# Up-projection of a ConvFFN: two buffers for a unit's evicted quarters, early history copies, the gated result in the tanh buffer, and put-off gates two units later

## The chip, the cores and the metric

The kernel runs on one core of one Trainium2 chip. The metric is the device time of one execution in microseconds (us); several executions are timed, and their median is quoted.

The core's engines, with the names that the profile uses: TensorE (PE; its weight loads are listed as PEld), VectorE (DVE), ScalarE (ACT), GpSimd (POOL) and SyncE (SP). Each takes its instructions in the order of its own queue. SyncE here only issues DMAs.

## The reference, cut to what matters

One layer: an input projection, an mLSTM group and an attention group, an output projection with a layer norm, then a ConvFFN with a layer norm. There are 2048 prompt tokens and 8 sequences of 16 new tokens, 1024 model columns and D_FF = 2816. The change lies in the ConvFFN:

```python
def conv_ffn(h, conv_prev, w_up, w_conv, b_conv, w_down):
    T = h.shape[1]
    u = h @ w_up                                    # value columns | gate columns, 2 * 2816
    ext = jnp.concatenate([conv_prev.astype(u.dtype), u], axis=1)
    c = b_conv + sum(ext[:, j:j + T] * w_conv[j] for j in range(CONV_W))   # causal, width 3
    a, g = jnp.split(c, 2, axis=-1)
    return (jax.nn.silu(g) * a) @ w_down, ext[:, -(CONV_W - 1):]
```

So each output token needs the two u rows before it: the history. For the prompt it comes from the token block before, for the 8 short sequences from a given state (`sconv`). All is computed in float32.

## The kernel before, in words

**Stages.** Input projection, mLSTM and attention chains woven with it, output projection, up-projection (`f_ups`), down-projection (`f_downs`). In the profile the up-projection lies at about 930 to 1900 us, the down-projection behind it.

**Loops of the up-projection.** Tokens are in three blocks b (`FBLOCKS`): 6, 6 and 5 tiles of 128 tokens; the last block holds four prompt tiles and the tile of the short sequences. In each block there are 22 units j (`NFF`), one for 128 value columns and the 128 gate columns that go with them. A unit (b, j) is computed as a Strassen-Winograd scheme of 2 x 2 blocks (value/gate columns by first/second half of the block's tokens): seven products s instead of eight. Each product is 12 matmuls (L1876): four steps of contraction, three matmuls for each, since float32 operands are split into a high and a low part (hh and hl for tokens, two halves of uw for weights). Products accumulate in three PSUM banks A, B and C. Units with even and odd j use different sets of banks, shown as fup and dps. The order of products is written out by hand: 6, 2, 5, product 1 of the next unit, 3, product 7 of the next unit, 4.

**Evictions (`f_after`, at most one set for each product).** For s = 1, ScalarE copies bank A to B (L1889). For s = 6, B is copied to a buffer u2 (L1901) before product 5 accumulates on B. For s = 2, A is copied into the tile u (L1903). For s = 5, B is copied to u4 (L1905), before product 3 accumulates on it, and VectorE adds u4 to bank C into u (L1906, and L1908 for the short sequences), before product 4 accumulates on C. For s = 3, B is copied into u (L1910, L1912). For s = 4, VectorE adds u2 to C into u (L1915). The tiles u, u2 and u4 have one buffer each.

**What follows in a unit, also in `f_after`.** GpSimd copies the history into the first two columns of u (L1916, and in block 2 L1918 for the short sequences), ScalarE computes the first tap of the convolution with its bias into cc (L1922), VectorE adds the other two taps (L1924; all three once for values and once for gates), and GpSimd saves the last two columns (L1925 to `prev`, L1927 to `convs`). In block 0 cc is stored to a DRAM buffer zc. In blocks 1 and 2 `f_gate` computes the gated result: tanh (L1946, into th), then two VectorE operations (L1947, L1948, the result into cc), then SyncE stores it to zf (L1949, L1951). Behind that, a put-off gate: the cc of a unit of block 0 is loaded back (L1939) and gated. This is done in units 0 to 17 of block 1 and in units 2 to 5 of block 2. The tile cc has two buffers, th has one.

**Work between the units.** `f_next` prepares the weights of later products: it casts the high part (ScalarE, L220) and subtracts it (VectorE, L221), stores what later blocks need again to zw, and loads it from there in blocks 1 and 2. At the turn of a block (the last unit of blocks 0 and 1) `f_tokens` forms the token operands hh and hl of the next block with the same L220 and L221 and some additions. `o_late` finishes two layer norms of the stage before, with a small tile of constants (`lnp`) in the pool f3.

**Down-projection.** `d_load` (L1993) loads the gated results from zf into tiles r, `d_weights` (L2011) loads the down weights (wdn, or sums of them, zt), `d_tokens` and the helper at L220/L221 split them, and `f_downs` runs the matmuls (L2080). The pools f2 (u, u2, u4 and four of the token operands) and f3 (`sconv`, `convs`, cc, th and others) are closed at its start and their space is given to r2, r3, r4 and yacc. `skew` only allocates padding, so that what follows lies at another address.

**Order.** TensorE's order is the program's order. For the other engines and for SyncE's DMAs a scheduler in the framework builds the queues from the program, so an edit can move instructions that it doesn't touch.

## Time and profile before

| | |
|---|---|
| timed runs | 2339.32, 2344.24 and 2351.91 us; median 2344.24 |
| profiled execution, its own time | 2340.57 us |
| its span in the profile | 2338.8 us |
| mean granted TensorE clock | 0.996 |
| TensorE busy | 2295.6 us (98%) |
| VectorE / ScalarE / GpSimd busy | 1803.8 (77%) / 1298.7 (56%) / 243.2 (10%) us |
| DMA | 624.98 MB, mean 267 GB/s |

The profile describes the profiled execution alone, in us from the start of its span. Busy times are sums over instructions. In rows of instructions the columns are start, duration, engine, line, operation, output <- inputs, shape, and in square brackets the idle time of the engine before the instruction, with what released it. In rows of windows they are the stretch and its length, the busy time of each engine with its number of instructions, the granted TensorE clock, the DMA engines' busy share, and GB/s. In rows of waits: who waited, for whom, total us, number of times, longest. In rows of groups: busy total and mean ns, then idle time before with what ended it. In rows of DMA issues: issues, KB each, median us from issue to landing.

### The profile page before, as it was taken

What the parts mean: (1) busy time and instruction counts of PE and PEld (TensorE: products, weight loads), DVE (VectorE), ACT (ScalarE), POOL (GpSimd) and SP (SyncE); (2) the same over time, 40 slices, a digit from 0 to 9 for tenths busy, and PEclk for the clock granted to TensorE, in tenths of its full rate; (3) what the DMA queues carried; (4) which work ended last, traced back from release to release, by engine and by line L of the source; (5) the groups of instructions that cost most, each with busy time, mean ns of one, the idle gap of its engine ahead of it and who ended that gap; (6) DMA issues with size and microseconds to landing.
All of it is one profiled execution on the core that took longest, in us unless ns stands there. A gap on an engine that the chain in (4) does not pass through costs nothing.

```text
span 2338.8 us, 39880 instructions
## 1 busy us (share of the span) xinstructions
PE 2295.6 (98%) x14425; PEld 2112.9 (90%) x14425; DVE 1803.8 (77%) x3150; ACT 1298.7 (56%) x2465; POOL 243.2 (10%) x298
## 2 busy tenths in 40 slices
PE   9999999999999999999999999999999999999998
PEld 8989998899887777999999999999999978888887
DVE  8676586796678898987788776778766777796897
ACT  5353466676666664655556455455545544554753
POOL 0101101101111221300001000002100100010100
PEclk9999999999999999999999999999999999999999
DMA  8798889889977667787776989878988776766763
GB/s 284 267 315 283 289 289 317 288 286 325 302 258 251 212 210 253 263 321 280 285 270 247 314 315 320 306 274 264 312 289 263 248 273 218 237 201 214 242 194 110
DMA packets 297365, 624.98 MB, mean 267 GB/s; under 512 B 47052, under 2 KB 140240, under 8 KB 297168
## 3 DMA queue, kind: packets, MB, share of 16 engines
q1 hardware_dynamic: 296304, 619.29, 77.7%
q10 hardware_dynamic: 864, 3.15, 0.4%
q8 instruction: 114, 1.87, 0.3%
q14 instruction: 83, 0.68, 0.1%
HBM read 451.78 MB, written 170.56 MB: 266 GB/s over the span
## 4 chain that ended last, share of the span: by engine, by line
PE 65%; DVE 9%; DMA 4%; ACT 3%; issue 3%; POOL 1%; SPq 0%; DVEq 0%; ACTq 0%; POOLq 0%
PE fup L1876 15%; PE dps L1876 15%; PE dps L2080 6%; PE fup L2080 6%; PE fht L2080 5%; PE dps L735 5%; PE dps L225 2%; DVE cc L1924 2%; PE dps L227 2%; PE dps L226 2%; DMA zf<-cc 1%; PE ppo L1371 1%; ACT cc L1922 1%; PE psc L1322 1%; DVE uw L221 1%
## 5 line engine op out<-in xcount | busy, mean ns | idle before, releaser
L1876 PE MATMUL dps<-hh,uw 128*128 128x384 f32 (+1 forms) x1848 | 479.1, 327 | 6.9 <-ACT u L1901 1.9
L1876 PE MATMUL fup<-hh,uw 128*128 128x384 f32 (+1 forms) x1848 | 477.5, 327 | 3.3 <-ACT u L1901 3.0
L1876 PEld LDWEIGHTS dps<-hh,uw 128*128 128x128 f32 x1848 | 329.3, 188 | 11.1 <-ACT u L1901 3.0
L1924 DVE SCALAR_TENSOR_TENSOR cc<-u,cw,cc 128x768 f32<-128x768 f32 (+1 forms) x264 | 252.5, 977 | 107.0 <-ACT cc L1922 102.2
L1876 PEld LDWEIGHTS fup<-hh,uw 128*128 128x128 f32 x1848 | 329.4, 188 | 4.9 <-ACT u L1901 3.8
L1876 PE MATMUL fup<-hl,uw 128*128 128x384 f32 (+1 forms) x924 | 301.3, 326 | 1.7 <-DVE hl L221 1.7
L1876 PE MATMUL dps<-hl,uw 128*128 128x384 f32 (+1 forms) x924 | 301.0, 326 | 0.0
L735 PE MATMUL dps<-w,oh 128*128 128x256 f32 x1344 | 253.8, 285 | 5.7 <-ACT zev L801 4.0
L221 DVE TENSOR_TENSOR w<-wraw,w 128x1024 fp32r<-128x1024 f32 (+2 forms) x163 | 188.2, 1160 | 61.2 <-ACT w L220 59.7
L220 ACT CAST w<-wraw 128x1024 fp32r<-128x1024 f32 (+2 forms) x163 | 161.0, 994 | 123.9 <-PE dps L735 58.8
L735 PEld LDWEIGHTS dps<-w,oh 128*128 128x128 f32 x1344 | 211.6, 190 | 18.1 <-issue 8.9
L220 ACT CAST uw<-wraw 128x1024 fp32r<-128x1024 f32 x126 | 123.4, 981 | 177.5 <-PE dps L2080 104.2
L1922 ACT ACTIVATE cc<-u,cw 128x768 f32<-128x768 f32 (+1 forms) x132 | 129.5, 997 | 122.2 <-DVE u L1915 62.2
L221 DVE TENSOR_TENSOR uw<-wraw,uw 128x1024 fp32r<-128x1024 f32 x126 | 142.4, 1131 | 64.9 <-ACT uw L220 64.8
L735 PE MATMUL dps<-w,ol 128*128 128x256 f32 x672 | 187.7, 279 | 0.0
L735 PE MATMUL dps<-oh,w 128*128 128x256 f32 x896 | 171.1, 284 | 5.8 <-ACT zev L801 1.6
L1876 PEld LDWEIGHTS fup<-hl,uw 128*128 128x128 f32 x924 | 173.5, 188 | 2.5 <-DVE hl L221 2.5
L1876 PEld LDWEIGHTS dps<-hl,uw 128*128 128x128 f32 x924 | 173.5, 188 | 0.0
L2080 PE MATMUL fup<-uw,fu 128*128 128x512 f32 x726 | 171.2, 392 | 2.0 <-DVE uw L221 2.0
L2080 PEld LDWEIGHTS fup<-uw,fu 128*128 128x128 f32 x726 | 137.2, 189 | 31.4 <-DVE uw L221 2.4
L2080 PE MATMUL dps<-uw,fu 128*128 128x512 f32 x660 | 160.7, 389 | 0.0
L735 PEld LDWEIGHTS dps<-oh,w 128*128 128x128 f32 x896 | 140.8, 188 | 12.4 <-issue 4.1
(337 smaller groups left out, 4621.1 us busy)
## 6 DMA issues: line engine op xcount, KB each, us to landing
uw<-zw SPq DMA_DIRECT2D x176, 512.0 KB, 4.9
zw<-uw SPq DMA_DIRECT2D x88, 512.0 KB, 3.0
w<-zws SPq DMA_DIRECT2D x72, 512.0 KB, 6.6
wv<-wup SPq DMA_DIRECT2D x66, 512.0 KB, 5.5
wraw<-wi SPq DMA_DIRECT2D x64, 512.0 KB, 5.2
wraw<-zt SPq DMA_DIRECT2D x60, 512.0 KB, 4.4
wraw<-wdn SPq DMA_DIRECT2D x45, 512.0 KB, 3.8
wraw<-wo SPq DMA_DIRECT2D x40, 512.0 KB, 4.6
```

Of the source, the lines that this page charges most:

```text
L220: nc.scalar.copy(hi, src)
L221: nc.vector.tensor_sub(lo, src, hi.bitcast(F32))
L225: mm(out, ah, bh, start=start, stop=False)
L226: mm(out, ah, bl, start=False, stop=False)
L227: mm(out, al, bh, start=False, stop=stop)
L735: mm(o, l, r, start=s in (1, 7) and c == k == i == 0, stop=k == 3 and i == 2, skip_group_check=True)
L1322: nc.tensor.matmul(ps[kvh][:, j, :nk], q[rs, j0 + j], k[rs, sel], start=i == 0, stop=i == 2)
L1371: nc.tensor.matmul(po[64 * kvh:64 * kvh + 64], w, pts[:, kvh], start=kt == 1, stop=kt == nk)
L1876: mm(ps, l[:, k], r[:, k], start=s in (1, 7) and k == 0 and i == 0, stop=k == 3 and i == 2, skip_group_check=True)
L1922: S.activation(c[:, v], u[:, v, 2:2 + n], AF.Identity, bias=w[3], scale=w[2])
L1924: V.scalar_tensor_tensor(c[:, v], u[:, v, i:i + n], w[i], c[:, v], op0=ALU.mult, op1=ALU.add)
L2080: mm(ps, l[:, k, c], r[:, k], start=s in (1, 4, 7) and u == 0 and k == 0 and i == 0, stop=u == nu - 1 and k == n - 1 and i == 2, skip_grou ...
```

## The change

- The tiles u, u2 and u4 get two buffers each instead of one.
- The two history copies of a unit are made when its tile u is allocated (at s = 6), not after its last eviction.
- The gated result is written over the tanh in th and stored from there, no longer written into cc; th gets two buffers.
- `sconv` and `convs` become the two halves of one tile `hist`. It is allocated in the middle of block 1, where the load of `sconv` moves too, and takes the place of the layer norm constants `lnp`.
- The put-off gates of block 0 are done in units 2 to 19 of block 1 instead of 0 to 17; those in block 2 stay.
- The padding behind the up-projection shrinks from 480 to 448 bytes per partition.

TensorE's instructions and their order are the same in both kernels, and each other engine has as many instructions as before.

```diff
--- before.py
+++ after.py
@@ -290,7 +290,7 @@
             self.f2, f2cm = enter("f2sb")
             self.f3, f3cm = enter("f3sb")
             self.f_ups(n)
-            self.skew(self.f2, 480)
+            self.skew(self.f2, 448)
             close(f3cm)
             close(f2cm)
             self.f2, f2cm = enter("dsb")
@@ -1672,7 +1672,7 @@
             yield
         for hf in range(2):
             c = slice(hf * 512, hf * 512 + 512)
-            gb = self.f3.tile([P, 2, 512], F32, name="lnp", tag="th", bufs=1)
+            gb = self.f3.tile([P, 2, 512], F32, name="lnp", tag="hist", bufs=1)
             for i, n in enumerate(("ln1_g", "ln1_b")):
                 nc.sync.dma_start(gb[:, i], self.a[n][:, c].to_broadcast([P, 512]))
             yield
@@ -1819,10 +1819,8 @@
 
     def f_ups(self, n):
         nc = self.nc
-        self.sconv, self.convs = [self.f3.tile([P, 2, NFF, DB, 2], F32, name=n_, tag=n_, bufs=1) for n_ in ("sconv", "convs")]
         for _ in range(AHEAD - n):
             self.f_next()
-        nc.sync.dma_start(self.sconv, self.a["sconv"].rearrange("p (v j) b r -> p v j b r", v=2))
 
         self.banks = [[pool.tile([P, 512], F32, name=n, tag=n) for _ in range(3)] for pool, n in ((self.fup, "fup"), (self.dps, "dps"))]
         self.f_written(0)
@@ -1835,6 +1833,10 @@
                 nxt = self.f_hT(b + 1)
             if i == 4:
                 self.f_written(1)
+            if (b, j, s) == (nb - 2, NFF // 2, 6):
+                hist = self.f3.tile([P, 2, 2, NFF, DB, 2], F32, name="hist", tag="hist", bufs=1)
+                self.sconv, self.convs = hist[:, 0], hist[:, 1]
+                nc.sync.dma_start(self.sconv, self.a["sconv"].rearrange("p (v j) b r -> p v j b r", v=2))
             self.f_product(b, j, s)
             while self.made < min(i + 1 + (AHEAD if b == 0 else AHEAD + 2), len(self.seq)):
                 self.f_next()
@@ -1891,8 +1893,11 @@
         if s == 7:
             return
         if s == 6:
-            u = f2.tile([P, 2, 770], F32, name="u", tag="u", bufs=1)
-            self.u = u, *[f2.tile([P, 384], F32, name=m, tag=m, bufs=1)[:, :h] for m in ("u2", "u4")]
+            u = f2.tile([P, 2, 770], F32, name="u", tag="u", bufs=2)
+            self.u = u, *[f2.tile([P, 384], F32, name=m, tag=m, bufs=k)[:, :h] for m, k in (("u2", 2), ("u4", 2))]
+            nc.gpsimd.tensor_copy(u[:, :, 0:2], self.prev[:, :, j])
+            if has_s:
+                nc.gpsimd.tensor_copy(u[:, :, 2 + WP:2 + n].rearrange("p v (b l) -> p v b l", b=DB)[:, :, :, 0:2], self.sconv[:, :, j])
         u, u2, u4 = self.u
         us = u[:, :, 2 + WP:2 + n].rearrange("p v (b l) -> p v b l", b=DB) if has_s else None
         m = WP - h
@@ -1913,9 +1918,6 @@
         if s != 4:
             return
         V.tensor_add(u[:, 1, 2:2 + h], C, u2)
-        nc.gpsimd.tensor_copy(u[:, :, 0:2], self.prev[:, :, j])
-        if has_s:
-            nc.gpsimd.tensor_copy(us[:, :, :, 0:2], self.sconv[:, :, j])
         c = self.f3.tile([P, 2, 768], F32, name="cc", tag="cc", bufs=2)[:, :, :n]
         for v in range(2):
             w = [self.cw[:, v * NFF + j, i:i + 1] for i in range(4)]
@@ -1932,7 +1934,7 @@
         self.f_gate(c, b, j, WP, n)
 
         i = (b - 1) * NFF + j
-        i = i if i < 18 else i - 6 if 24 <= i < 28 else None
+        i = i - 2 if 2 <= i < 20 else i - 6 if 24 <= i < 28 else None
         if b and i is not None:
             W0 = len(FBLOCKS[0]) * P
             c = self.f3.tile([P, 2, 768], F32, name="cc", tag="cc", bufs=2)[:, :, :W0]
@@ -1942,14 +1944,14 @@
     def f_gate(self, c, b, j, WP, n):
         nc, V = self.nc, self.nc.vector
         W = len(FBLOCKS[b]) * P
-        th = self.f3.tile([P, 768], F32, name="th", tag="th", bufs=1)[:, :n]
+        th = self.f3.tile([P, 768], F32, name="th", tag="th", bufs=2)[:, :n]
         nc.scalar.activation(th, c[:, 1], AF.Tanh, scale=0.5)
         V.scalar_tensor_tensor(th, th, 1.0, c[:, 1], op0=ALU.add, op1=ALU.mult)
-        V.tensor_mul(c[:, 0], th, c[:, 0])
-        nc.sync.dma_start(self.zf[b][j, :, :WP], c[:, 0, :WP])
+        V.tensor_mul(th, th, c[:, 0])
+        nc.sync.dma_start(self.zf[b][j, :, :WP], th[:, :WP])
         if n > WP:
             nc.sync.dma_start(self.zf[b][j, :, WP:].rearrange("p (b l) -> p b l", b=DB),
-                              c[:, 0, WP:].rearrange("p (b l) -> p b l", b=DB)[:, :, 2:])
+                              th[:, WP:].rearrange("p (b l) -> p b l", b=DB)[:, :, 2:])
```

## The prediction

> **What bounds the kernel now.** I read the page first, then the matrix engine's waits in the up-projection (930 to 1900 us of the span), then windows of single units, then the instructions around each stall.

> ```profile
> PE 2295.6 (98%) x14425; PEld 2112.9 (90%) x14425; DVE 1803.8 (77%) x3150; ACT 1298.7 (56%) x2465; POOL 243.2 (10%) x298
> ```

> TensorE (PE) is busy for 98% of the 2338.8 us span, so the change can only win back time in which TensorE stands still. It alters nothing TensorE executes. The list of what TensorE waited for in the up-projection is therefore nearly the ceiling:

> ```profile
> engine line waited for: us in total, times, longest us
> PE fup L1876 <- ACT u L1901: 3.0, 3, 1.2
> PE dps L1876 <- ACT u L1901: 1.9, 2, 1.3
> PE dps L1876 <- DVE u L1906: 1.7, 1, 1.7
> PE fup L1876 <- DVE hl L221: 1.7, 2, 1.5
> PE dps L1876 <- ACT uw L220: 1.4, 2, 0.7
> PE dps L1876 <- DVE u L1908: 0.8, 1, 0.8
> PE dps L1876 <- ACT u L1905: 0.7, 2, 0.5
> PE fup L1876 <- ACT u L1905: 0.2, 1, 0.2
> ```

> That is 11.4 us in 14 waits. Half of it (3.0 + 1.9 + 0.7 + 0.2 = 5.8) is for the evictions L1901 and L1905, which the change touches. The real loss is a little larger than each wait, since matmuls that otherwise overlap restart from nothing. Windows of whole units (of one block and column tile j) show it:

> ```profile
> core 0: us, PE busy (x) PEld busy (x) DVE busy (x) ACT busy (x) POOL busy (x), PEclk, DMA share, GB/s
> 1180.00:1194.56 14.56, 14.56 (x85) 14.56 (x85) 12.07 (x18) 8.10 (x15) 0.77 (x2) 1.00 0.72 272
> 1256.26:1272.41 16.15, 14.85 (x85) 14.54 (x85) 16.15 (x14) 12.42 (x15) 3.12 (x2) 1.00 0.68 237
> 1272.45:1288.50 16.05, 14.84 (x86) 14.52 (x85) 14.10 (x17) 7.48 (x11) 0.69 (x2) 1.00 0.65 214
> 1585.00:1601.00 16.00, 14.26 (x86) 13.89 (x85) 16.00 (x16) 12.02 (x16) 7.78 (x2) 1.00 0.60 193
> 1601.00:1614.30 13.30, 12.54 (x85) 12.28 (x84) 12.89 (x17) 6.67 (x12) 3.44 (x3) 1.00 0.77 246
> 1740.50:1752.82 12.32, 12.32 (x86) 12.32 (x86) 7.90 (x12) 6.04 (x12) 0.75 (x4) 1.00 0.82 248
> 1651.27:1715.86 64.59, 63.09 (x423) 61.61 (x422) 45.03 (x66) 32.39 (x63) 5.98 (x20) 1.00 0.90 302
> 1317.60:1392.60 75.00, 74.84 (x434) 74.02 (x434) 55.00 (x68) 38.28 (x63) 3.68 (x10) 1.00 0.88 307
> 938.90:956.80 17.90, 16.21 (x94) 15.40 (x93) 17.90 (x22) 13.11 (x18) 13.96 (x2) 1.00 0.71 241
> ```

> The first row is an undisturbed unit of blocks 0 and 1 (14.56 us, weight loads without a gap); the row 1740.50 is one of block 2 (12.32). Disturbed units are longer, and their weight loads (PEld) fall short by about the excess. At the turn from block 0 to 1 the excess is 16.15 − 14.56 = 1.59 and 16.05 − 14.56 = 1.49; at the turn from 1 to 2 it is 1.44 and 13.30 − 12.32 = 0.98. The five units (2,4) to (2,8) together lose 64.59 − 5 × 12.32 = 2.99. In (1,3) to (1,7) loads fall 0.98 short of the window. VectorE (DVE) has no idle time in the first and third of these turn units (16.15 of 16.15, 16.00 of 16.00), and little in the fourth.

> **Part by part.** All sums are against the profiled execution (2340.57 us, for a span of 2338.8).

> *Quarters u, u2, u4 in two buffers.* At the block turns the copy of one unit into u2 stands behind the conv tap of the unit before, because u2 is still held:

> ```profile
> 1260.45 1.02 ACT L1922 ACTIVATE cc<-u,cw 128x768 f32<-128x768 f32 x1
> 1261.38 0.46 ACT L1901 COPY u<-dps 128x384 f32<-128x384 f32 x1
> 1261.89 0.44 PE L1876 MATMUL dps<-hh,uw 128*128 128x384 f32 x1 [1.30 <-ACT u L1901]
> 1277.96 0.45 PE L1876 MATMUL fup<-hh,uw 128*128 128x384 f32 x1 [1.22 <-ACT u L1901]
> 1605.40 0.41 PE L1876 MATMUL fup<-hh,uw 128*128 128x320 f32 x1 [0.76 <-ACT u L1901]
> 1269.26 0.55 DVE L1906 TENSOR_TENSOR u<-dps,u 128x384 f32<-128x384 f32 x1
> 1270.34 0.33 PE L1876 MATMUL dps<-hh,uw 128*128 128x384 f32 x1
> ```

> In the changed program's queue the copy stands ahead of that tap (1.02) and of a cast of the next tokens, and needs only TensorE's own result. So all three waits for L1901 go. What is late next?
> - In (0,21) it is L1906, which must end before product 4 accumulates on its bank. It ends at 1269.26 + 0.55 = 1269.81, and that product began at 1270.34. VectorE has no idle time in this window, so L1906 doesn't come earlier with TensorE. Of 1.59 only 0.53 is won.
> - In (1,0) VectorE is idle for about 2 us, so all 1.49 is won; in (2,0) 0.98.
> - (0,1) has the same pattern with a wait that is in the 3.0 above; I put 0.4 on it.

> Sum: −3.4. The stall of (1,21), 1.7 us for L1906 on a VectorE that is full in that window (16.00 of 16.00), stays. So do those of the first unit (VectorE 17.90 of 17.90), and the two for L220.

> *Gated result in the tanh buffer, history copies at the start of the unit.* Both take something from in front of the conv tap L1922, behind which ScalarE's (ACT) evictions of the next unit queue:

> ```profile
> ACT cc L1922 <- POOL u L1918: 38.8, 20, 3.2
> ACT cc L1922 <- DMA zf<-cc: 18.7, 13, 3.5
> L1946 ACT ACTIVATE th<-cc 128x768 f32<-128x768 f32 x44 | 37.3, 847 | 37.9 <-DVE cc L1924 18.5 <-DVE cc L1948 17.8 <-DVE u L1908 1.3
> ```

> L1922 needed a cc buffer whose store to zf had not landed (18.7 us in 13 waits). With the result in th, cc is free when VectorE has read it, so these waits go. In block 2 the tap also waited in 20 of 22 units for GpSimd's (POOL) copy L1918, which came last of all in a unit; now it is made at the unit's start. TensorE felt both only where ScalarE's lag exceeded the slack of the next eviction: the 2.99 of (2,4) to (2,8) and up to 0.98 of (1,3) to (1,7), of which I take 0.8. The last unit has small waits of the same kind among the L1905 and L1908 rows; I take 0.5 of them. Sum: −4.3.

> The price is on the same engines. The put-off gates of block 0 come two units later: units 2 to 19 of block 1 instead of 0 to 17. Their instructions are as many as before. The two that move land in units with room (VectorE 55.00 of 75.00 us with such a gate in each). Two buffers of th let a second Tanh (0.85) stand directly behind the first, ahead of the L1905 copy. That is hidden by that copy's own slack of about 1.4 us in an undisturbed unit, and costs up to 0.85 per unit where the slack is used up. I take nothing.

> *Up-projection together:* −3.4 − 4.3 = −7.7. Bounds: nothing (the next wait takes over everywhere) and −15 (all 11.4 goes, with restarts).

> *Start of the down-projection.* The buffers f2 and f3 close there, and the order of SyncE's (SP) queue changes:

> ```profile
> 1889.36 9.11 SPq L1993 DMA_DIRECT2D r<-zf  x14
> 1906.03 1.57 SPq L2011 DMA_DIRECT2D wraw<-wdn  x2
> 1914.72 1.57 ACT L220 CAST uw<-wraw 128x1024 fp32r<-128x1024 f32 x2 [1.73 <-DMA wraw<-wdn]
> 1918.43 0.50 PE L2080 MATMUL fup<-uw,fu 128*128 128x512 f32 x1 [2.01 <-DVE uw L221]
> 1918.87:1922.28 3.41, 3.41 (x10) 2.66 (x9) 3.41 (x5) 0.00 (x0) 0.00 (x0) 0.50 0.98 362
> 1908.00:1916.00 8.00, 8.00 (x37) 6.62 (x36) 7.86 (x9) 2.96 (x4) 0.00 (x0) 1.00 1.04 410
> ```

> Fourteen loads r<-zf (9.11 us of issue) stand ahead of two loads of down weights. Those weights are cast late, and TensorE waits 2.01. Right behind that wait its granted clock is 0.50 for 3.41 us, in which it does 10 matmuls. At the pace of the last row (8.00 / 37 = 0.216) these take 2.16, so 1.25 more is lost. In the changed program one more load of down weights stands ahead of the fourteen, and it is the one this matmul needs. I take the wait and the slow stretch as gone and give back 0.3 at the next weight: −3.0. Bounds: nothing (another weight is late by as much), and −3.3.

> [...]

> **Sum:** −7.7 − 3.0 = −10.7, or 2329.9 against the profiled 2340.57. The median of the three runs is 2344.24, so 2333.5, said as 2333 (−0.46%).

> **The rivals.** *The down-projection's stall stays* and only the up-projection gains: 2344.2 − 7.7 = 2336.5. For it: each load there waits for space that the same last units free, and DMA is at its limit (share 1.04 in the 8 us before). Against it: the load's place in the queue.

> *More goes.* VectorE's lead at the block turns also grows, since less of its work waits for taps, and the L1906 waits shrink: 1.06 left in (0,21), 1.7 in (1,21), in all −13.5, so 2330.7. If the start and the L220 waits also eased, −15 − 3.3 gives 2326. Against it: VectorE has no gap in those windows, and its work there is unchanged.

> *The early history copies collide with VectorE.* A copy of four columns can be long:

> ```profile
> 939.30 12.62 POOL L1916 COPY u<-prev 128x4 f32<-128x4 f32 x1 [21.53 <-DVE ymix L1653]
> ```

> This one took 12.62 us while VectorE was busy without a gap. The copies now fall on busier stretches of VectorE. If each held VectorE for what it takes, 4 to 8 of them at the two turns at some 0.8 us (POOL's 3.12 and 7.78 us in the windows 1256 and 1585, against a quiet unit's 0.77, are already such lengthening) cost 3 to 6 of the 7.7: 2337 to 2340. Against it: the row shows the copy stretched, not VectorE.
> [...]

> *Slower: ScalarE's queue jams on the put-off gates.* ScalarE works in order. In 18 units of block 1 the second Tanh, on a tile loaded back from zc, stands ahead of the copies L1903 and L1905 on which the next products wait.

> ```profile
> cc<-zc SPq DMA_DIRECT2D x22, 768.0 KB, 5.3
> ```

> Its load takes 5.3 us from issue to landing. If it, or VectorE's gate two places earlier, lands after the Tanh's turn, everything behind is late by as much. Each unit pays what exceeds the slack of about 1.4. It decides from 10.7 / 18 = 0.6 us per unit; at 1.2 us per unit it costs 21.6 − 10.7 = 10.9 net, so 2355. Against it: before has the same loads, and no wait for cc<-zc is in ScalarE's list of waits.

> *It doesn't do what it says:* the copies stay behind casts that are due anyway, the waits for L1901 turn into waits for L1905 or L1906 of equal size, and only the block 2 part and half the rest are left: about −4, 2340.

> **How the numbers follow.** Forecast 0.38 (2333); stall of the down-projection stays 0.18; more goes 0.14; port collision or other waits in place of the old, together 0.15; slower 0.15. A difference of 0.5%, 11.7 us, is about what a measurement of this kernel can tell from no change. Faster by more than that is below 2332.5. The forecast lies at this bound, so half of its chance goes there, with all of "more goes" and a little of the rest: 0.37. Slower by over 0.5% needs the jam beyond 1.2 us a unit, or a similar one: 0.13. The rest, 0.50, is between. The range runs from 2324, where all waits and the clock stretch have gone (2326, with the spread of the runs), to 2348, where the jam about undoes the gain: 0.8 lies inside.

> **What would show it.** In the profile after, waits of L1876 for L1901 are gone, apart perhaps from hundredths; (1,0) and (2,0) last 14.56 and 12.32 us, (0,21) still some 15.6 with a wait for L1906; (2,4) to (2,8) last 61.6; ScalarE's waits for zf and for the history copy have left L1922; the matmul of the down-projection that waited 2.01 doesn't, and no 0.50 clock follows. Wrong would be the sum if waits for L1903 or L1905 appear all over block 1, if matmuls wait for a Tanh's tile behind a zc load, if history copies of over a microsecond stand before late taps, or if another weight load takes the place of the one I took as gone.

## The result, and the profile after

The changed kernel takes 2327.77 us (median of five runs, 2327.54 to 2334.69), the kernel before 2343.17 (five runs, two more than were known ahead, 2338.09 to 2351.91). The medians lie 15.4 us apart. The ratio of the two kernels' runs on record is 0.9951, with a 95% interval of 0.9935 to 0.9967: about 11.5 us faster, between 7.7 and 15.2. The forecast was 2333, with a range of 2324 to 2348. The profiled execution of the changed kernel took 2327.77 us, with a span of 2325.5 (2338.8 before).

In the changed kernel's file the evictions have other lines: matmul L1878, copy to u2 L1906, to u4 L1910, add on VectorE L1911, tap L1924, down-projection L2082. First a line of the page, then all that TensorE waited for from 930 to 1900 us (the third group is in the last unit):

```profile
PE 2292.0 (99%) x14425; PEld 2113.6 (91%) x14425; DVE 1803.0 (78%) x3150; ACT 1305.4 (56%) x2465; POOL 238.0 (10%) x298
```
```profile
engine line waited for: us in total, times, longest us
PE dps L1878 <- DVE u L1911: 2.6, 2, 1.7
PE dps L1878 <- ACT uw L220: 1.4, 2, 0.7
PE dps L1878 <- ACT u L1910: 1.1, 1, 1.1
PE fup L1878 <- DVE hl L221: 0.6, 2, 0.4
```

11.4 us of waits in the up-projection have become 5.7. No wait for the copy to u2 is left, nor one for the down weights. At the turn that copy now stands ahead of the conv tap in ScalarE's queue and starts when TensorE's product is there. The tap itself no longer waits for stores to zf or for GpSimd; in this stretch the only entry for it in ScalarE's list of waits is the last add of its unit:

```profile
1257.12 0.48 ACT L1906 COPY u<-dps 128x384 f32<-128x384 f32 x1 [3.54 <-PE dps L1878]
1258.89 1.03 ACT L1924 ACTIVATE cc<-u,cw 128x768 f32<-128x768 f32 x1
```
```profile
ACT cc L1924 <- DVE u L1920: 92.4, 59, 2.2
```

Windows of units that were shown of before, in order of time: (0,0), (0,21), (1,0), (1,21), (2,0), and (2,4) to (2,8):

```profile
core 0: us, PE busy (x) PEld busy (x) DVE busy (x) ACT busy (x) POOL busy (x), PEclk, DMA share, GB/s
938.56:955.46 16.90, 16.29 (x94) 15.47 (x93) 16.90 (x20) 12.54 (x18) 13.62 (x3) 1.00 0.62 216
1254.76:1270.56 15.80, 14.92 (x86) 14.60 (x85) 15.80 (x14) 12.32 (x15) 5.34 (x2) 1.00 0.72 255
1270.56:1285.06 14.50, 14.50 (x86) 14.50 (x85) 14.24 (x17) 7.41 (x11) 5.02 (x3) 1.00 0.68 208
1580.76:1596.76 16.00, 14.26 (x86) 13.90 (x85) 16.00 (x17) 12.01 (x16) 3.24 (x3) 1.00 0.62 198
1596.76:1609.06 12.30, 12.30 (x86) 12.30 (x85) 12.01 (x16) 7.60 (x13) 0.83 (x3) 1.00 0.77 251
1646.06:1707.66 61.60, 61.60 (x422) 61.60 (x421) 45.05 (x67) 33.72 (x63) 4.70 (x20) 1.00 0.95 315
```

(1,0), (2,0) and the five units of block 2 have no gap left in TensorE's weight loads. (0,21) and (1,21) keep theirs: VectorE is full in both windows. At the start of the down-projection SyncE's queue now has a load of down weights ahead of the fourteen loads:

```profile
1878.01 0.37 SPq L2013 DMA_DIRECT2D wraw<-wdn  x1
1878.98 9.99 SPq L1995 DMA_DIRECT2D r<-zf  x14
```

**A ledger by stage.** TensorE runs the same matmuls in the same order in both kernels, so the n-th matmul of one trace can be set against the n-th of the other. The table gives how much each stage of a kernel is longer or shorter than in the first profile of the kernel before (us, own alignment of the traces). "Ahead" is all that lies before unit (0,0); up to there every engine and SyncE run the same instructions in the same order in all kernels but the last two. "Turn 0→1" is (0,21) and (1,0), "tail" is (2,18) to (2,21) and what follows up to 1883 us, "down" the first 70 us of the down-projection. The last column goes to the last matmul. Stages that no kernel changes are left out of the columns. The labels are those of the experiments below.

| kernel | ahead | (0,0) | (0,1) | turn 0→1 | block 1 | (1,21) | (2,0) | (2,1)-(2,8) | tail | down | from (0,0) on |
|---|---|---|---|---|---|---|---|---|---|---|---|
| changed | -0.2 | -1.09 | -0.21 | -1.90 | -0.80 | 0.00 | -1.02 | -2.97 | -1.35 | -3.70 | -13.1 |
| changed, again | -1.9 | -1.35 | -0.20 | -1.91 | -0.80 | -0.02 | -1.01 | -2.98 | -1.34 | -3.78 | -13.4 |
| before, again | -0.2 | 0.00 | 0.02 | 0.00 | -0.40 | -0.01 | 0.00 | 0.95 | 0.00 | -0.24 | 0.3 |
| buffers alone (p_bufs) | 5.2 | -0.67 | -0.21 | -1.91 | 0.07 | -0.03 | -1.02 | -1.07 | -0.90 | -1.86 | -7.7 |
| gate alone (p_gate) | 0.4 | -0.26 | 0.00 | 0.01 | -0.80 | -0.03 | 0.03 | -0.02 | -0.01 | -1.86 | -3.0 |
| history alone (p_hist) | 2.9 | -1.55 | -0.01 | -0.04 | -0.09 | 0.00 | 0.00 | 0.63 | -1.04 | -3.76 | -5.9 |
| changed, one buffer (a_bufs1) | -1.8 | -0.03 | -0.01 | 0.00 | -0.80 | -0.03 | 0.03 | -2.98 | -1.03 | -3.79 | -8.6 |
| changed, gate in cc (a_gate) | 0.8 | -0.13 | -0.20 | -1.91 | -0.12 | -0.01 | -1.02 | -0.90 | -1.34 | -3.75 | -9.4 |
| changed, late history (a_hist) | -0.3 | -0.82 | -0.20 | -1.90 | -0.80 | -0.02 | -1.02 | 2.72 | -0.90 | -0.25 | -3.2 |
| changed, gates not shifted (a_shift0) | 2.4 | -0.60 | -0.20 | -1.91 | -0.80 | -0.01 | -1.01 | -2.24 | -1.33 | -3.68 | -11.8 |
| changed, plus order and GpSimd (a_best) | -1.0 | -0.42 | -0.19 | -2.76 | -0.80 | -2.02 | 0.40 | -2.98 | -1.33 | -3.52 | -13.6 |
| changed, plus order, no scaling (a_best2) | 4.1 | -1.36 | -0.20 | -2.75 | -0.80 | -1.99 | 0.37 | -2.97 | -1.34 | -3.79 | -14.8 |

Two columns, "ahead" and (0,0), vary though no edit but the last two touches what runs there. "Ahead" spreads over 7 us, more than any single part is worth, so the spans of single executions can't rank these kernels. The columns can, but those of block 1 and block 2 only with care: the kernel before differs from itself there by 0.40 and 0.95.

### The profile page after: what moved, and what is told of

It is laid out like the page before. It is cut to its first block, busy times and chain, and to the rows that moved or that the text cites. A ratio compares the mean times of both kernels' runs of the same rounds, so it can differ in the third digit from the quotient of the medians.

```text
span 2325.5 us, 39932 instructions
## 1 busy us (share of the span) xinstructions
PE 2292.0 (99%) x14425; PEld 2113.6 (91%) x14425; DVE 1803.0 (78%) x3150; ACT 1305.4 (56%) x2465; POOL 238.0 (10%) x298
## 4 chain that ended last, share of the span: by engine, by line
PE 73%; DVE 6%; issue 2%; DMA 2%; ACT 2%; POOL 0%; SPq 0%; DVEq 0%; ACTq 0%; POOLq 0%
PE dps L1878 18%; PE fup L1878 18%; PE dps L2082 6%; PE dps L735 6%; PE fht L2082 5%; PE fup L2082 5%; PE dps L225 2%; PE dps L227 2%; PE dps L226 2%; PE ppo L1371 1%; PE psc L1322 1%; PE ppt L1365 1%; PE dps L760 1%; DVE uw L221 1%; DVE w L221 1%
## 5 line engine op out<-in xcount | busy, mean ns | idle before, releaser
L1878 PE MATMUL dps<-hh,uw 128*128 128x384 f32 (+1 forms) x1848 | 477.5, 327 | 5.3 <-DVE u L1911 2.6
L1878 PE MATMUL fup<-hh,uw 128*128 128x384 f32 (+1 forms) x1848 | 476.4, 326 | 0.0
L1926 DVE SCALAR_TENSOR_TENSOR cc<-u,cw,cc 128x768 f32<-128x768 f32 (+1 forms) x264 | 257.6, 977 | 124.5 <-ACT cc L1924 121.0
L1878 PEld LDWEIGHTS dps<-hh,uw 128*128 128x128 f32 x1848 | 329.2, 188 | 7.6 <-DVE u L1911 3.2
L1878 PEld LDWEIGHTS fup<-hh,uw 128*128 128x128 f32 x1848 | 329.2, 188 | 0.0
L1878 PE MATMUL fup<-hl,uw 128*128 128x384 f32 (+1 forms) x924 | 301.3, 326 | 0.6 <-DVE hl L221 0.6
L1878 PE MATMUL dps<-hl,uw 128*128 128x384 f32 (+1 forms) x924 | 301.0, 326 | 0.0
L221 DVE TENSOR_TENSOR w<-wraw,w 128x1024 fp32r<-128x1024 f32 (+2 forms) x163 | 188.1, 1159 | 60.8 <-ACT w L220 59.5
L220 ACT CAST w<-wraw 128x1024 fp32r<-128x1024 f32 (+2 forms) x163 | 161.0, 993 | 122.0 <-PE dps L735 58.2
L220 ACT CAST uw<-wraw 128x1024 fp32r<-128x1024 f32 x126 | 123.2, 981 | 173.3 <-PE dps L2082 104.1
L221 DVE TENSOR_TENSOR uw<-wraw,uw 128x1024 fp32r<-128x1024 f32 x126 | 142.4, 1130 | 64.0 <-ACT uw L220 63.8
L1924 ACT ACTIVATE cc<-u,cw 128x768 f32<-128x768 f32 (+1 forms) x132 | 132.0, 1000 | 95.3 <-DVE u L1920 92.4
L1878 PEld LDWEIGHTS fup<-hl,uw 128*128 128x128 f32 x924 | 173.5, 188 | 1.4 <-DVE hl L221 1.4
L1878 PEld LDWEIGHTS dps<-hl,uw 128*128 128x128 f32 x924 | 173.5, 188 | 0.0
L2082 PE MATMUL fup<-uw,fu 128*128 128x512 f32 x726 | 169.1, 389 | 0.0
L2082 PEld LDWEIGHTS fup<-uw,fu 128*128 128x128 f32 x726 | 136.2, 188 | 28.3 <-ACT fht L2089 0.2
L2082 PE MATMUL dps<-uw,fu 128*128 128x512 f32 x660 | 160.9, 389 | 0.1
L735 PEld LDWEIGHTS dps<-oh,w 128*128 128x128 f32 x896 | 140.8, 188 | 12.3 <-issue 4.1
```

Source lines behind the costliest of these rows:

```text
L220: nc.scalar.copy(hi, src)
L221: nc.vector.tensor_sub(lo, src, hi.bitcast(F32))
L735: mm(o, l, r, start=s in (1, 7) and c == k == i == 0, stop=k == 3 and i == 2, skip_group_check=True)
L1878: mm(ps, l[:, k], r[:, k], start=s in (1, 7) and k == 0 and i == 0, stop=k == 3 and i == 2, skip_group_check=True)
L1924: S.activation(c[:, v], u[:, v, 2:2 + n], AF.Identity, bias=w[3], scale=w[2])
L1926: V.scalar_tensor_tensor(c[:, v], u[:, v, i:i + n], w[i], c[:, v], op0=ALU.mult, op1=ALU.add)
```

## The experiments

**One part alone.** Three kernels take one part of the change each and put it into the kernel before. The buffers of u, u2 and u4 were not tested apart from each other, nor the merged tile `hist` apart from the gate.

Buffers alone:
```diff
-self.skew(self.f2, 480)
+self.skew(self.f2, 448)
-u = f2.tile([P, 2, 770], F32, name="u", tag="u", bufs=1)
+u = f2.tile([P, 2, 770], F32, name="u", tag="u", bufs=2)
```
and `bufs=2` for u2 and u4.

> Before, with two buffers for u, u2 and u4 alone (and the padding of the change). Theory (each part has its own stalls): the block turns win, (1,0) 16.05 to 14.56 us, (2,0) 13.3 to 12.3, (0,21) about 0.5 shorter; ScalarE's waits of L1922 for zf stores and for the history copy stay, so (2,4) to (2,8) keep most of their 2.99 us; the down-projection's wait of 2.0 us and its half-clock stretch stay. Span about 3.5 to 4.5 us shorter than 2338.8. Rival (the buffers do everything in the up-projection): (2,4) to (2,8) last 61.6 as well and the span is about 8 shorter.

Measured: span 2336.3. The turns win all that they win in the changed kernel (−1.91, −1.02), and block 1 nothing (0.07). (2,1) to (2,8) win 1.07 of 2.97. TensorE still waits for the two copies, in block 2 (0.8) and in the last unit (0.7), and for the down weights. The half-clock stretch behind that last wait, which was expected to stay, did not come (down −1.86):

```profile
PE fup L2080 <- DVE uw L221: 2.0, 1, 2.0
PE fup L1876 <- ACT u L1901: 0.8, 2, 0.4
PE dps L1876 <- ACT u L1905: 0.7, 1, 0.7
```

Gate alone: th with two buffers, the product into th, the stores from there, and the merged tile `hist`, as in the change.

> Before, with the gated result in th (two buffers), stored from there, and sconv and convs in one tile in the middle of block 1, alone. Theory: L1922 no longer waits for zf stores (18.7 us before); (1,3) to (1,7) win 0.8, (2,4) to (2,8) about 1 to 2 of 2.99, block turns unchanged (within 0.3), the down-projection's wait stays. Span 1.5 to 3 us shorter. Rival (the buffers do everything): the units in blocks 1 and 2 stay as long as before, span within 0.5.

Measured: span 2336.1. Block 1 wins its whole 0.80, the turns nothing, as expected. Block 2 wins nothing (−0.02), where 1 to 2 us were expected: the tap there waits for the late history copy as before. Here too the wait for the down weights stays and the half-clock stretch doesn't come.

```profile
ACT cc L1924 <- POOL u L1920: 39.3, 21, 1.9
```

History alone: the two copies moved to where u is allocated.

> Before, with the two history copies at the start of the unit, alone. Theory: in block 2 L1922 no longer waits for L1918 (38.8 us before), VectorE's last tap comes earlier, (2,4) to (2,8) win 1 to 3 us; the block turns unchanged. In this program one more load of down weights stands ahead of the fourteen loads from zf, as in the changed kernel, so the 2.0 us wait and the half-clock stretch at the start of the down-projection go: 3.5 us. Span 4.5 to 6.5 shorter. Rival (the down-projection's gain comes from the buffers or the pools' sizes, not from the order of the loads): the wait there stays, span 1 to 3 shorter.

Measured: span 2335.8. The down-projection's wait is gone (−3.76), with nothing changed but the history copies, so the scheduler's new order of loads comes from them and not from the buffers or the pools. Block 2 was expected to win 1 to 3 us and lost 0.63. The tap no longer waits for GpSimd, but in the units with a put-off gate it waits for the store of cc, and a Tanh for the load of cc:

```profile
1661.36 0.85 ACT L1946 ACTIVATE th<-cc 128x768 f32<-128x768 f32 x1 [2.46 <-DMA cc<-zc]
1665.39 0.94 ACT L1922 ACTIVATE cc<-u,cw 128x656 f32<-128x656 f32 x1 [1.93 <-DMA zf<-cc]
1670.54 0.41 PE L1876 MATMUL dps<-hh,uw 128*128 128x320 f32 x1 [1.99 <-ACT u L1904]
```

(L1904 is the copy to u2 in this file.) One wait took the place of another.

**One part undone.** Four kernels take one part out of the changed one.

> The changed kernel with one buffer each for u, u2 and u4 (and the old padding). Compared unit by unit with the changed kernel, since stages ahead of the up-projection vary by several us between executions. Theory: the block turns' stalls for L1901 come back, (1,0) to 16.05, (2,0) to 13.3, (0,21) to 16.15, together 2.9 us; (1,3) to (1,7) and (2,4) to (2,8) stay clear, since the gated result in th and the early history copies have taken away what held the conv tap; the down-projection keeps its order of loads and no wait. Rival (block 2 needs the buffers too): (2,4) to (2,8) lose 1 to 3 us as well.

The edit is `bufs=1` for u, u2 and u4, and 480 for the padding. Measured: span 2328.7. The turns are back at the old length (0.00 and 0.03 in the table), block 1 and block 2 stay clear (−0.80, −2.98). So gate and history together do all of block 2, and the second buffers add nothing there.

> The changed kernel with the gated result written to cc and stored from there again (th keeps two buffers). Theory: L1922 waits for zf stores again, in block 1 and in the units of block 2 with a put-off gate; (1,3) to (1,7) lose about 0.8, (2,4) to (2,8) 1 to 2.5 us; turns and down-projection as in the changed kernel. Rival (two buffers of u hide the store): none of these units longer than in the changed kernel by more than 0.3.

```diff
-        V.tensor_mul(th, th, c[:, 0])
-        nc.sync.dma_start(self.zf[b][j, :, :WP], th[:, :WP])
+        V.tensor_mul(c[:, 0], th, c[:, 0])
+        nc.sync.dma_start(self.zf[b][j, :, :WP], c[:, 0, :WP])
```
(and the second store alike). Measured: span 2330.2. Block 1 loses 0.68 and block 2 2.07, near what was expected; the turns and the down-projection stay. But block 1 loses it in (1,17) and (1,19), not in (1,3) to (1,7), which stay clear, and block 2 loses it in (2,4) alone, where ScalarE waits 1.41 us for a zc load and TensorE 1.61 behind it. The waits for stores are back (22.9 us in 21 waits of the tap); which unit stalls for them is not fixed.

> The changed kernel with the two history copies after the last eviction again. Theory: L1922 waits for L1918 again in block 2 (some 36 us in 20 waits), (2,4) to (2,8) lose 1 to 3 us, turns unchanged; the order of the loads is as before again, so the down-projection's wait of about 2.0 us is back. A half-clock stretch behind that wait, which the execution of before had and the ones with the buffers alone and the gate alone did not, would add 1.6 to 1.9; I expect none. Rival (the late copies are hidden when u has two buffers): block 2 clear, only the down-projection's 2 us back.

Measured: span 2335.3. Block 2 loses 5.69 against the changed kernel, twice the most that was expected, and is 2.72 worse than before. One unit, (2,4), holds most of it:

```profile
1654.96 0.84 ACT L1948 ACTIVATE th<-cc 128x768 f32<-128x768 f32 x1 [2.53 <-DMA cc<-zc]
1655.71 0.41 ACT L1907 COPY u<-fup 128x320 f32<-128x320 f32 x1
1656.17 0.41 PE L1878 MATMUL fup<-hh,uw 128*128 128x320 f32 x1 [2.65 <-ACT u L1907]
```

(L1907 is the copy to u4 here.) ScalarE waits 2.53 us with the Tanh of a put-off gate for the load of its tile, the copy behind it is late, and TensorE waits 2.65: exactly the jam that the prediction gave as the way to a slower kernel. Behind this wait the granted clock fell as well, to 0.50 for 3.41 us from 1656.73 on, so the unit is 4.44 longer than in the changed kernel. It happens in block 2, where units are shorter, and not when all parts are there. The down-projection's wait is back too, and this time with a half-clock stretch (down −0.25), which was not expected.

> The changed kernel with the put-off gates back in units 0 to 17 of block 1. Theory: the shift moves two gates from units next to the block turn to undisturbed ones; (1,0) has 1.6 to 2 us of VectorE idle, a gate takes 1.9, so (1,0) or (1,1) may get a stall of 0 to 1 us; span 0 to 1 longer than the changed kernel's 2325.5. Rival (the shift is what frees the turn): (1,0) goes back to 16 us and block 1 gets waits for L1906 and L1910 again, span 2 to 3 longer.

The edit is the old line `i = i if i < 18 else ...`. Measured: span 2329.3, of which 2.6 us of the 3.8 more than in the changed kernel lie ahead, and from (0,0) on 1.3 more. The turns and block 1 are the same to 0.01, so the shift of the put-off gates is worth nothing there; neither a stall in (1,0) nor the rival's came. 0.74 is lost in one unit of block 2, (2,7), whose ScalarE waited for a load of up weights. One execution can't say whether that is the shift's doing.

**The two kernels profiled again.**

> The kernel before, unchanged, profiled again: which of the differences between executions are not the change's. If the stalls are fixed by the queues' order, the units at the block turns, in block 1 and in (2,4) to (2,8) last what they did in the first profile within 0.3 us in all, and the down-projection's wait of 2.0 us is there. What varies between executions should vary here as well: the stages ahead of the up-projection by up to 5 us, the first unit (0,0) by up to 1.6, and the half-clock stretch behind the wait, which two of four executions with the wait have had. Rival: the first unit and the stages ahead repeat within 0.2, and then their differences are the edits' doing.

> The changed kernel, unchanged, profiled again. Theory: from unit (0,2) on it repeats its first profile within 0.3 us, without the down-projection's wait and without a half-clock stretch; (0,0) between 16.4 and 18 us by the time at which the load of cw lands, later cw, longer unit. Rival: (0,0) is 16.87 again whatever that load does.

Measured: the changed kernel repeats itself to 0.02 in every column from (0,1) to the tail, and to 0.08 in the down-projection. The kernel before repeats its turns, but its block 1 was 0.40 shorter and its block 2 0.95 longer, more than the 0.3 expected. In (2,5) ScalarE now waited 1.45 us for a zc load, which it did not in the first profile, and TensorE 1.68 behind it in (2,6). So its stalls hang on when stores and loads land, and single values of these two columns under about 1 us show little. What can be read is whether a column is empty of stalls. Block 1 is 0.80 shorter in all eight executions that store the gated result from th, and never in the other four besides the first (−0.40 to 0.07). Block 2 is 2.97 or 2.98 shorter in five of the six that have that and the early history copies, 2.24 in the sixth (a_shift0), and at most 1.07 shorter in the rest. The changed kernel has lost the stalls and with them the variation. The first unit was the same in both profiles of before (0.00), not different by up to 1.6, and is looked at below.

**Two attempts at what is left.**

> The changed kernel with two more edits, aimed at what is left: in the last unit of a block the operands of product 2 of the next block are split after product 5's evictions, not before, which puts L1911 ahead of two splits in VectorE's queue; and the small scaling of cw, for whose load VectorE stands idle 2.3 us at 895 in the changed kernel, is done by GpSimd. Theory (a full VectorE queue is what holds L1911 at the turns and the first units): (0,21) 15.74 to 14.56, (1,21) 16.0 to 14.6, (0,0) 1 to 2 us shorter; together 3 to 4.5 us, 0.9932 to 0.9937 of before. Rival (the queue is full whatever its order, and another eviction or split is late next): less than 1 us, or waits for hl of the next block's product 2 or 6 take the place.

```diff
-{1: (1, "t1", "t3"), 7: (7, "t2"), 6: (6,), 2: (2,), 5: (5, "t4"), 3: (3,), 4: (4,)}
+{1: (1, "t1", "t3"), 7: (7, "t2"), 6: (6,), 2: (), 5: (2, 5, "t4"), 3: (3,), 4: (4,)}
-nc.vector.tensor_scalar_mul(self.cw[:, :NFF], self.cw[:, :NFF], 0.5)
+nc.gpsimd.tensor_scalar_mul(self.cw[:, :NFF], self.cw[:, :NFF], 0.5)
```

Measured: 2327.6 us, 0.9950 of before (0.9931 to 0.9970). Both turn units lose their stall: (0,21) 15.74 to 14.56, (1,21) 16.03 to 14.01. In (0,21) L1911 now runs at 1264.28 us, ahead of three splits; in the changed kernel it ran at 1267.77, behind two of them. So L1911 was held by its place in the queue. But (2,0) gets 1.42 back, with a wait of 1.1 for VectorE's add for the short sequences, and (1,0) 0.33. The net is 1.5 us of the 3 to 4.5. The other edit moved a wait, and (0,0) took 17.53 us, not 1 to 2 less than 16.87. GpSimd scales cw when it lands, and the next statistic of a layer norm, for which VectorE waits, now stands behind it:

```profile
899.26 0.44 POOL L1704 TENSOR_SCALAR cw<-cw 128x88 f32<-128x88 f32 x1 [7.96 <-DMA zh<-ymix]
899.67 0.57 POOL L1579 TENSOR_TENSOR lsc<-lsc,mhalf 128x1 f32<-128x1 f32 x1
900.27 1.28 DVE L1592 SCALAR_TENSOR_TENSOR ymix<-ymix,lsc,o_ln_b 128x1024 f32<-128x1024 f32 x1 [2.89 <-POOL lsc L1579]
```

> The changed kernel with the order at the block turns of the version before (product 2 of the next block split after product 5's evictions), and without the scaling of cw: the factor 0.5 is applied in the gate's second VectorE operation instead, so VectorE waits for no load of cw at about 898. Theory: VectorE's full queue from there to the first unit starts 2 to 3.5 us earlier, the waits for hl in (0,0) go, (0,0) comes to 15.6 to 16.6 us (17.95 before, 17.5 with the scaling on GpSimd, where VectorE waited for GpSimd's lsc instead); the turns are as in the version before, (0,21) 14.56 and (1,21) 14.0 with 13.7 for (2,0). Against the changed kernel 1.5 to 3 us shorter from (0,0) on; 0.993 to 0.9945 of before. Rival: the start waits for something else, a cast on ScalarE or another load, and (0,0) stays above 17.

```diff
-nc.vector.tensor_scalar_mul(self.cw[:, :NFF], self.cw[:, :NFF], 0.5)
-        V.tensor_mul(th, th, c[:, 0])
+        V.scalar_tensor_tensor(th, th, 0.5, c[:, 0], op0=ALU.mult, op1=ALU.mult)
```
(with the order of a_best). Measured: 2328.86 us, 0.9944 of before (0.9930 to 0.9958). The first unit comes to 16.59 us, at the edge of what was expected, and from (0,0) on this is the shortest kernel: 14.8 less than before, 1.4 to 1.7 less than the changed one. Its stages ahead were 4.1 us longer in the profiled execution. In the timed runs neither version can be told from the changed kernel, whose interval covers both.

## Why the prediction was right

It forecast −10.7 against the profile, and the ledger from (0,0) on says −13.1; the timed ratio gives −11.5 (−7.7 to −15.2). Term by term:

| term | forecast | measured |
|---|---|---|
| (0,21), (1,0), two buffers | −0.53 − 1.49 | −1.90 |
| (0,1), two buffers | −0.4 | −0.21 |
| (2,0), two buffers | −0.98 | −1.02 |
| block 1, gate in th | −0.8 | −0.80 |
| (2,4) to (2,8), gate and history | −2.99 | −2.97 |
| last units | −0.5 | −1.35 |
| start of the down-projection | −3.0 | −3.70 |
| (1,21), and the first unit (0,0) | 0 | 0.00, and −1.09 |

**The mechanism in the up-projection is shown.** The turns' stalls come and go with the second buffers alone (p_bufs, a_bufs1), those of block 1 with the gate in th alone (p_gate, a_gate). That block 1 was worth 0.80 is in part luck: the second profile of before had only half of it, and a_gate had its stalls in other units. Block 2 the prediction ascribed to gate and history without asking whether one is enough. It isn't: alone they bring −0.02 and +0.63, neither of which is more than before differs from itself (0.95), together −2.98. Behind the tap's wait for the history copy there lay the one for the store, so each removed alone leaves the other: with the gate alone the tap waits 42.4 us for the copy (38.8 before), with the history alone 21.7 us for stores (18.7 before). The 1.07 that the second buffers alone bring there is about as much as before differs from itself, so it may be nothing. The three parts alone add up, in (2,1) to (2,8), to −0.46.

**One reading was wrong.** The prediction put 0.4 on (0,1), for a wait for L1901 that it took to be within the 3.0. But the three waits of that row lie in (1,0), (2,0) and (2,4) (1.22, 0.76 and 1.02), and in (0,1) TensorE waits for a cast of weights (0.71). The unit won 0.21 with the second buffers all the same; by what isn't shown.

**L1911 on a full VectorE stays,** as said:

```profile
1268.37 0.45 PE L1878 MATMUL dps<-hh,uw 128*128 128x384 f32 x1 [0.88 <-DVE u L1911]
```

a_best showed that this is the order in the queue, not the amount of work alone: the same work in another order cleared both units and uncovered the next add at (2,0).

**The tail was sized too small:** the prediction took 0.5 of the last unit's waits for L1905 and L1908, which were 0.52 and 0.84. The buffers alone win 0.90 there and the history copies alone 1.04; both together 1.35.

**The down-projection: right about the queue, half wrong about the clock.** The wait goes with the order of loads: it is gone in all eight executions that have the new order, and is there in all five that have the old one (before twice, p_bufs, p_gate, a_hist). But the prediction took the half-clock stretch to belong to the wait. With a wait of the same length, the buffers alone had none. Three of the five executions with the wait had the stretch, none of the eight without it.

The traces show what it goes with. In all 13 of them the granted clock changes only at multiples of 3.41333 us from one another (to 0.004 us): in before it falls at 120.042, 161.002, 266.815 and 1918.866 us, 12, 31 and 484 steps apart, and in the changed kernel at 119.671, 160.631, 266.444 and 293.751, 12, 31 and 8 apart. The grid lies at another place in each execution. The rows are steps of that grid, the one that holds the wait and the next one: before (its next step is in the prediction), a_hist, p_bufs and p_gate.

```profile
1915.46:1918.87 3.41, 1.40 (x7) 0.85 (x6) 3.38 (x4) 2.65 (x4) 0.00 (x0) 1.00 1.04 415
```
```profile
1912.73:1916.14 3.41, 1.40 (x6) 1.03 (x6) 3.38 (x5) 1.78 (x2) 0.00 (x0) 1.00 0.87 323
1916.14:1919.55 3.41, 3.41 (x9) 2.66 (x9) 3.41 (x5) 0.00 (x0) 0.00 (x0) 0.50 0.86 308
```
```profile
1913.97:1917.39 3.42, 1.60 (x8) 0.98 (x6) 3.39 (x4) 2.23 (x3) 0.00 (x0) 1.00 1.04 417
1917.39:1920.80 3.41, 3.22 (x14) 2.68 (x15) 3.41 (x5) 0.00 (x0) 0.00 (x0) 1.00 0.70 247
```
```profile
1913.32:1916.73 3.41, 2.28 (x10) 1.42 (x8) 3.38 (x5) 2.30 (x3) 0.00 (x0) 1.00 1.03 410
1916.73:1920.14 3.41, 2.69 (x12) 2.23 (x13) 3.41 (x5) 1.05 (x1) 0.00 (x0) 1.00 1.01 380
```

In before, in its second profile and in a_hist the whole wait, 2.01 us (3.41 − 1.40), lies in one step, and the next step runs at 0.50. In p_bufs it is spread over two steps (1.82 and 0.19), in p_gate too (1.13 and 0.72), and the clock stays. Over the 13 traces, from 300 us to the last matmul, all five steps in which TensorE stood idle for 1.88 us or more were followed by a step at 0.50, of the 14 with 1.5 to 1.82 us two, of the 68 with 0.9 to 1.5 us none. In before the step with 2.01 us of idle time was, the one with the next most, 1.42 us, wasn't; in the changed kernel the most is 1.33 us, and no step from 300 us to the last matmul is at 0.50. So in these five executions the wait cost clock where it fell into one step. The prediction counted the stretch without knowing that, from one execution, and here it was lucky: in two of the five it isn't there. What sets the grid's place isn't shown.

Its sizes: set against p_bufs matmul by matmul, the stretch costs 1.60 us in before (1.63 and 1.62 in the other two), not 1.25. The 10 matmuls that the prediction counted in it, and the 37 from which it took a pace of 0.216, include some that lie only partly in the window; from start to start one takes 0.227. The wait is worth 1.9, with the 0.25 that the next weights take back already off, where the prediction had 2.01 − 0.3. The rest of the 3.70, 0.2, is a delay at 1901 us that the second profile of before doesn't have.

**The first unit hangs on a load that no edit touches.** From the scaling of cw, at about 898 us, to the end of unit (0,0) VectorE stands idle for some 0.5 us at most, and its splits (hl) are what TensorE waits for in (0,0). The scaling waits for the load of cw. What counts is how long ahead of (0,0) it runs. In order of that lead in us, with what (0,0) won: 40.06 (0), 40.09 (0), 40.12 (−0.03), 40.19 (−0.13), 40.30 (−0.26), 40.66 (−0.60), 40.74 (−0.67), 40.86 (−0.82), 41.14 (−1.09), 41.41 (−1.35), 41.73 (−1.55). These are before again, before, a_bufs1, a_gate, p_gate, a_shift0, p_bufs, a_hist, changed, changed again and p_hist, all executions that scale cw on VectorE: a microsecond of lead wins about a microsecond, and kernels that share a part stand far apart in this order. With the load out of the way (a_best2) the unit wins 1.36 and the wait for hl falls to 0.2. Two executions of one kernel lie close together (0.03 and 0.27 of lead), so an influence of the edits on when the load lands isn't ruled out. The prediction forecast nothing for this unit. Without its 1.1 to 1.35 the change's own part, from (0,0) on, is about 12, of which 1.6 hangs on the clock stretch. That lies within the interval of the timed ratio, 7.7 to 15.2.

**The rivals.** That the down-projection's stall stays, that nothing is gained, and that more goes at the turns by itself: all refuted by the table. The collision of the history copies with VectorE: the copies did get long (GpSimd was busy for 5.34 and 5.02 us in the windows of the turn), but the turns won what was forecast, and VectorE's four splits beside these copies (from 1264.43 to 1272.17 us) took 1.75 us each, as did the two without a copy beside them (at 1259.23 and 1275.84), so VectorE didn't pay:

```profile
1264.67 3.23 POOL L1898 COPY u<-prev 128x4 f32<-128x4 f32 x1 [12.17 <-DVE cc L1926]
1268.44 6.13 POOL L1927 COPY prev<-u 128x4 f32<-128x4 f32 x1 [0.55 <-DVE u L1911]
```

The jam on put-off gates: not in the changed kernel, where no wait of ScalarE for a zc load is listed, but real in block 2. ScalarE waited over a microsecond there for a zc load in five executions (before again 1.45, p_bufs 1.89, a_gate 1.41, p_hist 2.46, a_hist 2.53), and TensorE up to 2.65 us behind it. Each of the five lacks the gate in th or the early history copies. The prediction's argument against the jam, that before has no such wait, held for the first profile of before and not for the second.

## What to carry to other kernels

Where several conditions hold the same instruction, removing one of them may bring nothing or a loss; read what the instruction would wait for next, and remove them together. An edit of a few tiny copies can move transfers in another stage through the scheduler, so compare the DMA queue's order before costing a change. Set stages side by side, matmul by matmul, when the span varies by more than the change is worth.
